# Wider modulation columns, another order of products and an earlier gate on the output weights, in an fp32 hybrid block on one core

## The chip, the cores and the metric

One NeuronCore of a Trainium2 chip runs the whole program. The metric is device time in microseconds (us). The kernel before took 2079.22 us, the median of 3 runs (2076.57 to 2082.44). A core has a matrix engine (PE, with its weight loads listed as PEld), three elementwise engines (DVE, ACT, POOL), and SP, which here only issues transfers; each takes its instructions in the order in which they are written for it, and waits on semaphores for the others.

## The reference

One layer on 1024 tokens with model width 1024, all in float32. The modulation vector is a product of the conditioning c with a 1024 x 6144 matrix, cut into six vectors of 1024.

```python
mod = c @ w_ada + b_ada       # shift, scale, gate for each of the two sub-layers
h = rms_norm(x) * (1 + scale) + shift
z = h @ w_in                  # q, k, v of both mixers, their gates, two branch gates
y_a = diff_attention(...)     # 8 heads, softmax(q1 k1) - lam * softmax(q2 k2), causal
y_b = mlstm_chunkwise(...)    # 4 heads
merged = sigmoid(g_A) * (y_a @ w_a) + sigmoid(g_B) * (y_b @ w_m)
x = x + gate * (merged @ w_out)
h2 = rms_norm(x) * (1 + scale2) + shift2
x = x + gate2 * (relu(h2 @ w_ff1) ** 2 @ w_ff2)     # width 4096
```

(The lines are a shortened form; `...` stands for the projected columns.)

## The kernel before

**Arithmetic.** Every float32 operand is split into a high and a low part (ACT copies the high part, line 320 in `parts`; DVE subtracts it, line 138), and a product is three matrix products: high by high, high by low, low by high (`mm_block`, line 328). Most large products use a scheme with seven block products instead of eight. Each left and right operand of the seven, named 1 to 7, is a block or a sum or difference of blocks, made on DVE before it is split; the results are added up on DVE as they come out of PSUM (lines 313 and 316 are the helpers `sub` and `add`). Products 1 and 2 give the first output block, 3 and 4 end the second and third, 6 or 7 the fourth.

**Stages, in order of time.** Input norm and the first modulation columns; from about 60 us the *token-major* units (`Tok`: five units of seven products of 48 matmuls with 256 columns) with the rest of the modulation woven in; then `Conv` and `Gate` units with 512 columns (from 306.92 us); the four mLSTM heads; the eight attention heads, with the products by w_m in the last; the products by w_a, the merge of both branches and the product by w_out (`Chunks`, seven products of 48 matmuls with 512 columns); the first feed-forward matrix in groups (`Ff1`, g0 to g15); the second one (28 products of 48 matmuls) with the residual added in.

**Modulation.** `ada_unit` makes 256 of the 4096 remaining columns: two loads of 512 KB into one buffer (`cr[1]`, named crow), eight DVE operations of 128x256 that multiply a row block with its entry of c and add (lines 715 and 717), a product with a matrix of ones that sums over the partitions (tile adp, lines 725 and 731). A load and all its eight operations are one entry of the list `extra`, put between two products; 14 of the 16 units fit there, two are put between the parts of the mLSTM heads.

**Order of work.** Nothing reorders instructions at run time: the order in which the Python functions call the engines is the order of each engine's queue. `weave` puts filler steps between main steps. Loads are issued from SP, in order as well: one that waits for a buffer holds up those behind it. Buffers come from pools by tag ("r", "v", "e", "u", "f", "m"); a new tile of a tag waits until the oldest one is free. `Chunks.prep` splits the operands of the next product, `Chunks.run` does the matmuls.

**Output gate.** The rows of w_out are loaded in pieces (line 1631) and multiplied by the gate (tile gta, line 1664) just ahead of the splits that use them. **Feed-forward.** A group's four result blocks are squared ReLUs; seven blocks or sums of them go to DRAM (act_d) as left operands of the second matrix. At the seam between the two matrices the first operands (act, tag "r") and the residual (xn_d, four loads of 1 MB into acc, line 2011) are loaded while the last group ends.

Of the kernel before, what the change touches and what calls it, by code (L numbers as in the profile page):

```python
# [36 lines left out]
def kernel(  # L37
# [40 lines left out]
    ub_d = dp.tile([AH, S + P], F32, name="ub_d")  # L78
    ea_d = dp.tile([32, S], F32, name="ea_d")
# [195 lines left out]
    def run(steps):  # L275
        for f in steps:
            f()
# [66 lines left out]
    class Group:  # L344
# [20 lines left out]

        def load_first(self):
# [32 lines left out]
        def weights(self, order):  # L399
# [3 lines left out]
            for q, i in enumerate(order):  # L403
# [7 lines left out]
                if i == 7:  # L411
# [200 lines left out]
    def gate_rows(gps):  # L612

        gs = wt("b", [16, S], "gs")
        for i in range(2):
            nc.scalar.copy(gs[:, i * 512:(i + 1) * 512], gps[i][0:16, :])
        nc.sync.dma_start(gs_d, gs)
# [77 lines left out]
    def ada_unit(u):  # L695

        c0 = 2048 + u * 256
        box = []

        def gather():  # L700
            ab = wt("f", [P, 2, 256], "ac")
            ac = ab[:, 0]
            box.append(ab)
            if u < 4 or u >= 12:
                nc.sync.dma_start(
                    ab[:, 1], bass.AP(tensor=b_ada.tensor, offset=b_ada.offset + c0, ap=[[0, P], [1, 256]])
                )
            src = w_ada[0][:, c0:c0 + 256].rearrange("(k p) c -> p k c", p=P)
            for q in range(2):
                stv = cr[1].rearrange("p (k c) -> p k c", k=4)  # L710
                nc.sync.dma_start(stv, src[:, q * 4:q * 4 + 4, :])
                for k in range(4):
                    kk = q * 4 + k
                    if kk == 0:
                        nc.vector.tensor_scalar(ac, stv[:, k, :], cond[:, 0:1], None, op0=ALU.mult)
                    else:
                        nc.vector.scalar_tensor_tensor(  # L717
                            ac, stv[:, k, :], cond[:, kk:kk + 1], ac, op0=ALU.mult, op1=ALU.add
                        )

        def total():
            ac, br = box[0][:, 0], box[0][:, 1]
            ps = bank("pa", "adp")
            if u < 4 or u >= 12:
                nc.tensor.matmul(ps[:, 0:256], lhsT=ones, rhs=ac, start=True, stop=True)
                nc.vector.tensor_tensor(br, ps[:, 0:256], br, op=ALU.add)
                i, cc = (0, u * 256) if u < 4 else (1, (u - 12) * 256)
# [97 lines left out]
    class Tok(Group):  # L825
# [13 lines left out]
        def s3(self):  # L839
            return cr[0].rearrange("p (k c) -> p k c", k=4)  # L840
# [1232 lines left out]
```

## Time and profile before

| what | value |
|---|---|
| median of 3 runs | 2079.22 us |
| the profiled execution's own time; its span; clock | 2075.06 us; 2073.0 us; 0.979 of full speed |
| PE busy | 1989.1 us, 96% of the span |
| DVE busy | 1655.4 us, 80% |
| ACT busy | 1045.0 us, 50% |
| POOL busy | 59.3 us, 3% |
| moved by DMA | 296.71 MB, mean 143 GB/s |

PE is nearly always busy by this count, but a matmul counts as busy for longer where the clock is low or where it follows a gap, so the count of matmuls in a stretch tells more than the busy share: in an undisturbed stretch with 512 columns there are 219 in 50 us, that is 0.228 us for each. The granted clock (PEclk) is 1.00 at 2.4 GHz and falls towards 0.5 at 1.2 GHz.

### The profile page before, as it was taken

To read this page: it belongs to the slowest core of one execution; us is meant where nothing else is said; L and a number is where in the kernel's file an instruction comes from. 1 tells how busy PE (TensorE), PEld (TensorE's weight loads), DVE (VectorE), ACT (ScalarE), POOL (GpSimd) and SP (SyncE) were. 2 spreads that over 40 slices of the span, in tenths; PEclk is the share of its full clock that TensorE was granted. 3 is DMA by queue.
4 is the path that set the end of the run, shared out by engine and by line. 5 is a ranking of instruction groups with operands and counts; after the bars stand their busy time and mean duration, and the time that the engine had idled before them with its cause. 6 is when DMAs were issued, how large, how long until landed. Compare 5 with 4: busy or idle time off the path is not lost.

```text
span 2073.0 us, 30238 instructions
## 1 busy us (share of the span) xinstructions
PE 1989.1 (96%) x11201; PEld 1723.2 (83%) x11201; DVE 1655.4 (80%) x2964; ACT 1045.0 (50%) x1966; POOL 59.3 (3%) x154
## 2 busy tenths in 40 slices
PE   5899999999999999999999899999899999999999
PEld 5899998888787899999999788777678887788887
DVE  7976768889676568999978657999867667998896
ACT  5522324544566557877767634456445445433332
POOL 0000000000011000000000110000000000000000
PEclk7999999999999999999999999999999999999999
DMA  8354452333765442322222665513444446744532
GB/s 283 107 173 157 146 180 101 102 112 134 219 207 169 138 126 54 85 77 82 62 64 85 198 226 168 185 41 112 162 153 153 146 148 235 275 154 159 163 107 77
DMA packets 210633, 296.71 MB, mean 143 GB/s; under 512 B 14067, under 2 KB 132494, under 8 KB 210486
## 3 DMA queue, kind: packets, MB, share of 16 engines
q1 hardware_dynamic: 207542, 285.35, 43.2%
q0 software_dynamic: 2944, 9.44, 1.2%
q8 instruction: 88, 1.44, 0.3%
q14 instruction: 59, 0.48, 0.1%
HBM read 206.43 MB, written 79.93 MB: 138 GB/s over the span
## 4 chain that ended last, share of the span: by engine, by line
PE 62%; DVE 15%; DMA 11%; issue 6%; ACT 4%; POOL 1%; SPq 0%; DVEq 0%; POOLq 0%; ACTq 0%
PE cps L328 15%; PE pb L328 8%; PE pc L328 7%; PE pa L328 7%; PE pd L328 4%; DMA crow<-in_w_ada_dram 4%; PE ps L166 3%; PE ps L165 3%; PE ps L167 3%; PE lg L1190 3%; PE pv L1243 3%; DVE ac L717 2%; DMA ex<-ea_d 1%; PE tp L1223 1%; PE ops L579 1%
## 5 line engine op out<-in xcount | busy, mean ns | idle before, releaser
L328 PE MATMUL cps<-t_op,s_op 128*128 128x512 f32 x2016 | 471.9, 395 | 10.6 <-ACT s_op L320 5.2
L328 PEld LDWEIGHTS cps<-t_op,s_op 128*128 128x128 f32 x2016 | 379.1, 189 | 100.8 <-ACT s_op L320 6.5
L320 ACT ACTIVATE w_op<-w_st 128x512 fp32r<-128x512 f32 (+1 forms) x192 | 130.6, 695 | 179.8 <-PE pb L328 62.6
L138 DVE TENSOR_TENSOR w_op<-w_st,w_op 128x512 fp32r<-128x512 f32 (+1 forms) x192 | 144.3, 770 | 8.3 <-ACT w_op L320 6.4
L165 PE MATMUL ps<-w_hi,hT 128*128 128x256 f32 x512 | 146.5, 286 | 0.0
L166 PE MATMUL ps<-w_lo,hT 128*128 128x256 f32 x512 | 145.9, 285 | 0.0
L167 PE MATMUL ps<-w_hi,hT 128*128 128x256 f32 x512 | 145.7, 284 | 0.0
L320 ACT ACTIVATE s_op<-act 128x1024 fp32r<-128x1024 f32 x56 | 58.6, 1052 | 143.4 <-PE cps L328 107.6
L328 PE MATMUL pc<-bt,w_op 128*128 128x512 f32 x384 | 99.8, 407 | 6.1 <-ACT w_op L320 5.1
L1200 ACT ACTIVATE ee<-ee,mneg 128x256 f32<-128x256 f32 (+7 forms) x128 | 98.2, 769 | 9.8 <-DVE mneg L1196 9.5
L1190 PE MATMUL lg<-kb,qe 128*128 128x512 f32 (+3 forms) x384 | 96.7, 360 | 3.2 <-DVE mneg L1196 2.5
L166 PEld LDWEIGHTS ps<-w_lo,hT 128*128 128x128 f32 x512 | 97.6, 191 | 1.3 <-issue 0.9
L165 PEld LDWEIGHTS ps<-w_hi,hT 128*128 128x128 f32 x512 | 97.6, 191 | 0.5
L167 PEld LDWEIGHTS ps<-w_hi,hT 128*128 128x128 f32 x512 | 97.6, 191 | 0.3
L328 PEld LDWEIGHTS pc<-bt,w_op 128*128 128x128 f32 x384 | 73.7, 195 | 27.2 <-ACT w_op L320 6.0
L328 PE MATMUL pa<-b,w_op 128*128 128x512 f32 x384 | 94.3, 396 | 0.7 <-DVE w_op L138 0.7
L316 DVE TENSOR_TENSOR acc<-cps,acc 128x512 f32<-128x512 f32 x116 | 76.9, 684 | 13.6 <-PE cps L328 13.5
L328 PEld LDWEIGHTS pa<-b,w_op 128*128 128x128 f32 x384 | 72.7, 190 | 16.1 <-DVE w_op L138 1.0
L717 DVE SCALAR_TENSOR_TENSOR ac<-crow,cond,ac 128x256 f32<-128x256 f32 x112 | 54.0, 482 | 29.5 <-DMA crow<-in_w_ada_dram 27.8
L1196 DVE CUSTOM_DVE_ANT_0 ee<-lg,bs 128x512 f32<-128x512 f32 (+4 forms) x128 | 69.9, 559 | 8.8 <-PE lg L1190 7.8
L138 DVE TENSOR_TENSOR s_op<-act,s_op 128x1024 fp32r<-128x1024 f32 x56 | 68.2, 1219 | 5.9 <-ACT s_op L320 5.9
L1190 PEld LDWEIGHTS lg<-kb,qe 128*128 128x128 f32 x384 | 61.5, 192 | 11.0 <-DVE mneg L1196 6.3
(406 smaller groups left out, 4798.8 us busy)
## 6 DMA issues: line engine op xcount, KB each, us to landing
w_st<-in_w_in_dram SPq DMA_DIRECT2D x72, 512.0 KB, 4.4
act<-act_d SPq DMA_DIRECT2D x56, 512.0 KB, 4.4
w_st<-in_w_ff_dram SPq DMA_DIRECT2D x36, 512.0 KB, 4.1
crow<-in_w_ada_dram SPq DMA_DIRECT2D x32, 512.0 KB, 4.2
w<-in_w_ff_dram SPq DMA_DIRECT2D x32, 512.0 KB, 4.9
act_d<-s SPq DMA_DIRECT2D x48, 256.0 KB, 2.0
wa<-in_w_ada_dram SPq DMA_DIRECT2D x16, 512.0 KB, 4.8
mq_d<-cv SPq DMA_DIRECT2D x16, 512.0 KB, 2.6
```

Source lines behind the costliest of these rows:

```text
L138: return (nc.gpsimd if pool else nc.vector).tensor_tensor(dst, src, hi.bitcast(F32), op=ALU.subtract)
L165: nc.tensor.matmul(o, lhsT=ah, rhs=bh, start=first, stop=False)
L166: nc.tensor.matmul(o, lhsT=ah, rhs=bl, start=False, stop=False)
L167: nc.tensor.matmul(o, lhsT=al, rhs=bh, start=False, stop=last)
L316: (nc.gpsimd if pick(pool, n) else nc.vector).tensor_tensor(o, a, b, op=ALU.add)
L320: nc.scalar.activation(dst[0], src, AF.Copy)
L328: nc.tensor.matmul(ps, lhsT=p, rhs=q, start=first and k == 0 and r == 0, stop=k == 3 and r == 2, skip_group_check=True,)
L717: nc.vector.scalar_tensor_tensor(ac, stv[:, k, :], cond[:, kk:kk + 1], ac, op0=ALU.mult, op1=ALU.add)
L1190: nc.tensor.matmul(lg[:, 0:max(256, w)], lhsT=hd["q"][hf][e][:, r, q4 * P:(q4 + 1) * P], rhs=hd["k"][e][:, c0:c0 + max(256, w)], start=r = ...
L1196: nc.vector.tensor_tensor_reduce(ee[:, c0:c0 + w], lg[:, 0:w], hd["bs"][:, n - c0 - w:n - c0][:, ::-1], -0.125, first, ALU.add, ALU.min, last,
L1200: nc.scalar.activation(ee[:, 0:n], ee[:, 0:n], AF.Exp, bias=mneg[:, e:e + 1], scale=-1.0, accum_out=ssum[:, e:e + 1])
L1243: nc.tensor.matmul(pv[:, 0:256], lhsT=pts[kk // 4][r][:, (kk % 4) * P:(kk % 4 + 1) * P], rhs=v, start=kk == 0 and r == 0, stop=kk == qi an ...
```

## The change

Six places are edited.

1. *Modulation.* Eight units of 512 columns. A load of 512 KB now holds two row blocks of 512 columns; the loads go to two buffers in turn, each is issued two products before its two DVE operations (128x512), and the product by ones comes one product after the last of them. All 32 loads lie in the token-major stage and the first `Conv` unit; the mLSTM heads have none. Where the gate needs its bias, this is a load of its own.
2. *Token-major units.* Products in the order 1, 2, 5, 6, 3, 7, 4; the left operand of 7 is made in place of a block; product 5's result is copied by ACT. The first unit's loads and splits stand between the calls that make its right operands.
3. *Output weights.* During the last attention head the rows of w_out are loaded (8 x 512 KB, buffer "u"), multiplied by the gate on DVE and stored to wo_d; later `pieces` loads from there.
4. *First feed-forward matrix, start.* For g0 to g3 the square of the first block is made by ACT; g0's and g1's sums of blocks are made two at a time in groups 6 and 8 from reloaded blocks; all eight evictions of the second half of the normed input go to ACT.
5. *Last group.* Order 1, 6, 5, 3, 7, 4, 2; its sums are made after the second matrix's ninth product.
6. *Residual.* The four loads of xn_d go; after the 10th, 11th, 12th and 14th of the second matrix's 28 products, POOL issues one transfer of 1 MB each that adds it to an accumulator in place (`accum_op`). The first seven products go in the order 1, 2, 7, 4, 5, 6, 3, and their results are copied by ACT where nothing is to be added.

```diff
@@
+        def fetch(q):
+            stv = cr[q % 2].rearrange("p (k c) -> p k c", k=2)
+            src = w_ada[0][q * 256:(q + 1) * 256, c0:c0 + 512].rearrange("(k p) c -> p k c", p=P)
+            nc.sync.dma_start(stv, src)
...
+            for k in range(2):
+                f = cond[:, q * 2 + k:q * 2 + k + 1]
+                if q or k:
+                    nc.vector.scalar_tensor_tensor(ac, stv[:, k, :], f, ac, op0=ALU.mult, op1=ALU.add)
+                else:
+                    nc.vector.tensor_scalar(ac, stv[:, k, :], f, None, op0=ALU.mult)
@@
+        def p5(self):
+            for n in self.ns:
+                self.pb[n] = bank("pa", "pb5")
+                self.m7[n] = wt("m", [P, 512], "m7")
+                self.prod(5, n, self.pb[n], True)
+                nc.scalar.activation(self.m7[n], self.pb[n], AF.Copy)
@@
     right(7, "vvvv")
+    first_tok.load()
     right(5, "eeee")
+    first_tok.weights(ORDER_T[0:2])
     half(1)
     gate_rows(gps)
     right(6, "rrrr")
+    first_tok.weights(ORDER_T[2:6])
     right(4, "rruu")
+    first_tok.weights(ORDER_T[6:])
...
+    for u, (fetch, gather, total) in enumerate(ada):
+        for q in range(4):
+            extra[2 + u * 4 + q].append(lambda f=fetch, q=q: f(q))
+            extra[4 + u * 4 + q].insert(0, lambda f=gather, q=q: f(q))
+        extra[8 + u * 4].insert(0, total)
@@
-        more = ada[na + h::MH]
-        for u, (gather, total) in enumerate(more):
-            filler.insert(len(filler) * (2 * u + 1) // (2 * len(more) + 1), gather)
-            filler.insert(len(filler) * (2 * u + 2) // (2 * len(more) + 1), total)
@@
+            def gate_wo(r):
+                w = wos.pop(r)
+                nc.vector.tensor_tensor(w, w, gta, op=ALU.mult)
+                nc.sync.dma_start(wo_d[r * P:(r + 1) * P, :], w)
+
+            for r in range(8):
+                units[12 + 2 * r] = lambda r=r, f=units[12 + 2 * r]: (fetch_wo(r), f())
+                units[15 + 2 * r] = lambda r=r, f=units[15 + 2 * r]: (gate_wo(r), f())
@@
-            wo = pieces("e", "wo", w_out[0], False, (11,), behind)
+            wo = pieces("e", "wo", wo_d, False, (11,))
@@
+        elif g.g in (6, 8):
+            fetch, one, two = late_sums(groups[LATE[g.g // 2 - 3]])
+            g.weights((1, 7, 2, 5, 6, 3, 4))
+            run([fetch, g.p1, g.p7, g.p2, g.p5, one, g.p6, two, g.p3, g.p4])
@@
-        if i == 1 and c == 0:
-            nc.scalar.activation(au[:, j], ps, AF.Copy)
+        if c == 0 and i not in (5, 6):
+            nc.scalar.activation(d[:, j], ps, AF.Copy)
@@
-    for q, t0, c0 in ((aa, 0, 0), (ab, 0, 512), (ac, 512, 0), (av, 512, 512)):
-        nc.sync.dma_start(q, xn_d[t0:t0 + 512, c0:c0 + 512].rearrange("(t p) c -> p t c", p=P))
...
+    joins = {9: ((aa, 0, 0),), 10: ((ac, 512, 0),), 11: ((av, 512, 512),), 13: ((ab, 0, 512),)}
     for n in range(7 * NC):
...
+        if n == 8:
+            groups[-1].sums()
+        for q, t0, c0 in joins.get(n, ()):
+            nc.gpsimd.dma_start(
+                q, xn_d[t0:t0 + 512, c0:c0 + 512].rearrange("(t p) c -> p t c", p=P), accum_op=ALU.add
+            )
```

DVE's queue before, in the first token-major unit: the modulation's operations (crow, cond to ac) between weight splits (w_op), weight sums (w_st) and result sums (m).

```order
L715 TENSOR_SCALAR ac<-crow,cond 128x256
L138 TENSOR_TENSOR w_op<-w_st,w_op 128x1024
L717 SCALAR_TENSOR_TENSOR ac<-crow,cond,ac 128x256 x3
L138 TENSOR_TENSOR w_op<-w_st,w_op 128x1024
L313 TENSOR_TENSOR crow<-w_st 128x1024
L316 TENSOR_TENSOR m_917<-pb_982,m_917 128x512
L717 SCALAR_TENSOR_TENSOR ac<-crow,cond,ac 128x256 x3
L316 TENSOR_TENSOR m_944<-pb_1008,m_944 128x512
L717 SCALAR_TENSOR_TENSOR ac<-crow,cond,ac 128x256
L316 TENSOR_TENSOR w_st<-w_st 128x1024
L138 TENSOR_TENSOR w_op<-w_st,w_op 128x1024
L316 TENSOR_TENSOR m_797<-pd,m_797 128x512
```

The same place in the changed kernel; the second product's split (w_op) already stands well ahead of these rows.

```order
L317 TENSOR_TENSOR c<-pb_907,m_800 128x512
L317 TENSOR_TENSOR c<-pb_934,m_827 128x512
L723 TENSOR_SCALAR ac<-crow,cond 128x512
L317 TENSOR_TENSOR w_st<-w_st 128x1024
L721 SCALAR_TENSOR_TENSOR ac<-crow,cond,ac 128x512
L139 TENSOR_TENSOR w_op<-w_st,w_op 128x1024
L317 TENSOR_TENSOR m_908<-pc,m_908 128x512
L721 SCALAR_TENSOR_TENSOR ac<-crow,cond,ac 128x512
L317 TENSOR_TENSOR m_908<-m_908,m_800 128x512
L317 TENSOR_TENSOR m_935<-pc,m_935 128x512
L721 SCALAR_TENSOR_TENSOR ac<-crow,cond,ac 128x512
L317 TENSOR_TENSOR m_935<-m_935,m_827 128x512
```

The operations are twice as wide and half as many, and one or two, not up to three or five, stand between two result sums.

DVE's queue before, at the end of the feed-forward groups g0 and g1: s are the sums that go to DRAM, s_15345 is the left operand of product 7 of g2, and its split (w_op) is what PE needs next.

```order
L316 TENSOR_TENSOR c<-c,m_15085 128x512
L316 TENSOR_TENSOR m_14855<-pc,m_14855 128x512
L313 TENSOR_TENSOR s_15270<-c,a_15227 128x512
L313 TENSOR_TENSOR s_15289<-a_15247,c 128x512
L313 TENSOR_TENSOR s_15270<-m_14855,s_15270 128x512
L316 TENSOR_TENSOR c<-c,m_15109 128x512
L316 TENSOR_TENSOR m_14870<-pc,m_14870 128x512
L313 TENSOR_TENSOR s_15294<-c,a_15247 128x512
L313 TENSOR_TENSOR s_15345<-w_st 128x512
L316 TENSOR_TENSOR w_st<-w_st 128x4x128
L313 TENSOR_TENSOR s_15294<-m_14870,s_15294 128x512
L138 TENSOR_TENSOR w_op<-s_15345,w_op 128x512
```

And now, where s_15254 is the left operand of product 7 of g2:

```order
L139 TENSOR_TENSOR w_op<-w_st,w_op 128x512
L317 TENSOR_TENSOR c<-pb_15082,m_14786 128x512
L139 TENSOR_TENSOR w_op<-w_st,w_op 128x512
L317 TENSOR_TENSOR c<-pb_15096,m_14801 128x512
L314 TENSOR_TENSOR s_15254<-w_st 128x512
L317 TENSOR_TENSOR w_st<-w_st 128x4x128
L139 TENSOR_TENSOR w_op<-s_15254,w_op 128x512
```

The sums and the second block's additions no longer stand between the last c of g1 and the operand of g2.

DVE's queue now, in the last attention head, where nothing of w_out stood before: wor is a row block of w_out, sg the products by w_m, ee, ssum and ptl the softmax.

```order
L1257 TENSOR_TENSOR ptl<-tp,pth 128x512
L1284 TENSOR_TENSOR yt<-yt,ssy 128x512
L1235 RECIPROCAL ssum<-ssum 128x2
L1257 TENSOR_TENSOR ptl<-tp,pth 128x128
L1236 SCALAR_TENSOR_TENSOR ssum<-ssum,nlam 128x1
L1541 TENSOR_TENSOR wor<-wor,gta 128x1024
L1239 SCALAR_TENSOR_TENSOR ee<-ee,ssum 128x768
L1541 TENSOR_TENSOR wor<-wor,gta 128x1024
L139 TENSOR_TENSOR w_lo<-w_st,w_hi 128x1024
L1320 SCALAR_TENSOR_TENSOR sg<-sg,ps 128x512
L139 TENSOR_TENSOR w_lo<-w_st,w_hi 128x1024
```

Each wor row waits for a load that was issued three steps earlier, and the softmax stands behind it.

## Rows read from the trace of the kernel before

**Rows 1.** The page: PE's busy time with its share of the span and instructions, and the shares of the chain that ended last, by engine.

```profile
PE 1989.1 (96%) x11201; PEld 1723.2 (83%) x11201; DVE 1655.4 (80%) x2964; ACT 1045.0 (50%) x1966; POOL 59.3 (3%) x154
...
PE 62%; DVE 15%; DMA 11%; issue 6%; ACT 4%; POOL 1%; SPq 0%; DVEq 0%; POOLq 0%; ACTq 0%
```

**Rows 2.** The view of windows, by stage: window, its length, then for PE, PEld, DVE, ACT and POOL the busy time (and instructions), the granted clock, the busy share of the DMA engines, GB/s.

```profile
60.00:310.00 250.00, 234.48 (x1853) 229.79 (x1852) 184.08 (x305) 76.81 (x108) 3.43 (x6) 0.96 0.50 155
310.00:540.00 230.00, 230.00 (x1016) 188.57 (x1015) 193.98 (x249) 108.35 (x155) 0.00 (x0) 1.00 0.39 131
...
1100.00:1180.00 80.00, 74.23 (x437) 64.46 (x437) 69.40 (x180) 58.67 (x137) 4.88 (x8) 0.94 0.47 146
1180.00:1300.00 120.00, 119.29 (x555) 98.66 (x554) 76.83 (x106) 49.92 (x79) 8.13 (x14) 1.00 0.59 195
1300.00:1400.00 100.00, 94.75 (x401) 75.35 (x400) 98.84 (x126) 46.41 (x66) 1.85 (x2) 0.98 0.32 108
1400.00:1500.00 100.00, 91.70 (x408) 73.22 (x407) 87.81 (x144) 55.84 (x102) 3.27 (x3) 0.95 0.41 137
...
1510.00:1740.00 230.00, 230.00 (x1001) 186.60 (x1000) 159.56 (x251) 114.53 (x189) 0.00 (x0) 1.00 0.44 151
1740.00:1800.00 60.00, 54.65 (x226) 42.56 (x225) 52.68 (x60) 27.43 (x34) 0.00 (x0) 0.97 0.88 313
...
1800.00:1850.00 50.00, 50.00 (x219) 40.86 (x218) 47.23 (x55) 19.32 (x22) 0.00 (x0) 1.00 0.52 168
```

**Rows 3.** The view of PE's waits from 60 to 310 us: what waited, for what; us in total, times, the longest.

```profile
PE pb L328 <- DVE m L316: 6.6, 2, 3.9
...
PE adp L731 <- DVE ac L717: 1.8, 2, 1.4
```

**Rows 4.** The same for DVE, from 60 to 310 us.

```profile
DVE ac L717 <- DMA crow<-in_w_ada_dram: 26.5, 12, 3.5
DVE ac L715 <- DMA crow<-in_w_ada_dram: 18.0, 9, 3.0
```

**Rows 5.** The view of windows, ten microseconds at the start of the token-major stage (columns as in group 2).

```profile
80.00:90.00 10.00, 4.05 (x25) 3.65 (x23) 10.00 (x14) 5.45 (x10) 0.00 (x0) 0.71 0.39 113
```

**Rows 6.** The timeline of PE at the start of the token-major stage: start, length, engine, line, operation, names and shapes, number, and in brackets the idle time before and what ended it.

```profile
75.56 6.02 PE L328 MATMUL pa<-w_op,hT 128*128 128x256 f32 x49
...
87.92 7.10 PE L328 MATMUL pa<-w_op,hT 128*128 128x256 f32 x46 [4.33 <-DVE w_op L138]
```

**Rows 7.** The same view at the end of the stage, where the first `Conv` product begins.

```profile
306.92 2.91 PE L328 MATMUL pa<-hT,w_op 128*128 128x512 f32 x12
```

**Rows 8.** The timeline of DVE at the start of the token-major stage.

```profile
78.08 1.09 DVE L604 TENSOR_SCALAR mo<-mo 128x512 f32<-128x512 f32 x3
...
86.64 1.22 DVE L138 TENSOR_TENSOR w_op<-w_st,w_op 128x1024 fp32r<-128x1024 f32 x1
```

**Rows 9.** The chain that ended last, in order of time (start, length, what), one whole product of the token-major stage.

```profile
203.99 5.77 PE pd L328 x48
```

**Rows 10.** The view of the tile crow: line, engine, operation, names, number: shortest, median, longest in ns, first and last start, shapes.

```profile
L717 DVE SCALAR_TENSOR_TENSOR ac<-crow,cond,ac x112: 474/484/487, 99.1 to 621.6; 128x256 f32<-128x256 f32 x112
L789 DVE SCALAR_TENSOR_TENSOR cv<-crow,par_v,cv x48: 1274/1278/1286, 326.0 to 508.0; 128x1023 f32<-128x1023 f32 x16, 128x1022 f32<-128x1022 f32 x16, 128x1021 f32<-128x1021 f32 x16
```

**Rows 11.** The view of the tile adp, columns as above.

```profile
L725 PE MATMUL adp<-ac,ksq x16: 377/377/484, 129.2 to 626.0; 128*128 128x256 f32 x16
```

**Rows 12.** The chain in the first mLSTM head.

```profile
567.81 3.95 DMA crow<-in_w_ada_dram
```

**Rows 13.** The view of line 1664, the output weights by the gate.

```profile
L1664 DVE TENSOR_TENSOR wo<-wo,gta x8: 1216/1226/1227, 1283.6 to 1329.3; 128x1024 f32<-128x1024 f32 x8
```

**Rows 14.** The view of windows in the last attention head.

```profile
1200.00:1210.00 10.00, 10.00 (x46) 8.27 (x45) 7.83 (x10) 3.82 (x6) 0.54 (x1) 1.00 0.99 348
```

**Rows 15.** PE's waits from 1300 to 1400 us.

```profile
PE cps L328 <- ACT t_op L320: 2.7, 1, 2.7
PE cps L328 <- DVE t_op L138: 2.5, 3, 1.5
```

**Rows 16.** PE's waits from 1400 to 1500 us, the two largest of g2's product 7 and 6.

```profile
PE pc L328 <- ACT w_op L320: 3.8, 1, 3.8
...
PE pd L328 <- ACT w_op L320: 1.1, 1, 1.1
```

**Rows 17.** The timeline of DVE there: the last c of g1, and the left operand of product 7 of g2.

```profile
1476.53 0.68 DVE L316 TENSOR_TENSOR c<-pb,m 128x512 f32<-128x512 f32 x1
...
1482.54 0.69 DVE L313 TENSOR_TENSOR s<-w_st 128x512 f32<-128x512 f32 x1
```

**Rows 18.** The view of windows there.

```profile
1480.00:1490.00 10.00, 6.25 (x16) 4.39 (x15) 8.83 (x15) 4.24 (x8) 0.00 (x0) 0.68 0.99 339
```

**Rows 19.** PE's waits from 1740 to 1800 us, the seam of the two feed-forward matrices.

```profile
PE cps L328 <- ACT s_op L320: 5.2, 3, 2.4
```

**Rows 20.** The chain at the seam.

```profile
1768.23 11.42 DMA act<-act_d
```

**Rows 21.** The page: transfers by queue (q0 holds those that POOL issues) with packets, MB and their share of 16 engines over the span.

```profile
q0 software_dynamic: 2944, 9.44, 1.2%
```

**Rows 22.** The page: transfers of one kind, with their number, KB each and us from issue to landing.

```profile
wo<-in_w_out_dram SPq DMA_DIRECT2D x8, 512.0 KB, 5.2
...
acc<-xn_d SPq DMA_DIRECT2D x4, 1024.0 KB, 9.4
```

More of the change, by code (lines that the diff above doesn't have):

```diff
@@ new lines, in gather @@
+        def gather(q):
+            stv = cr[q % 2].rearrange("p (k c) -> p k c", k=2)
+            if not q:
+                box.append(wt("f", [P, 512], "ac"))
+            ac = box[0]
+            for k in range(2):
[4 more added lines that the diff above has]
+                    nc.vector.tensor_scalar(ac, stv[:, k, :], f, None, op0=ALU.mult)
+            if gate and q == 3:
+                br = wt("f", [P, 512], "br")
+                nc.sync.dma_start(br, bass.AP(tensor=b_ada.tensor, offset=b_ada.offset + c0, ap=[[0, P], [1, 512]]))
+                box.append(br)
@@ L721, in total @@
         def total():
-            ac, br = box[0][:, 0], box[0][:, 1]
+            ac = box[0]
             ps = bank("pa", "adp")
[L724 to L727, printed above, removed]
-                nc.gpsimd.dma_start(gt_d[i, :, cc:cc + 256], br)
+            if gate:
+                br = box[1]
+                nc.tensor.matmul(ps, lhsT=ones, rhs=ac, start=True, stop=True)
+                nc.vector.tensor_tensor(br, ps, br, op=ALU.add)
+                i, cc = (0, u * 512) if u < 2 else (1, (u - 6) * 512)
+                nc.gpsimd.dma_start(gt_d[i, :, cc:cc + 512], br)
@@ L729, in total @@
             else:
-                for t in range(2):
+                for t in range(4):
                     nc.tensor.matmul(
@@ L1441 @@
         del behind[:]
-        u.all([lambda n=n: run(steps[n * len(steps) // 4:(n + 1) * len(steps) // 4]) for n in range(4)] + [lambda: None] * 3)
+        steps = [lambda v=steps[n * len(steps) // 4:(n + 1) * len(steps) // 4]: run(v) for n in range(4)]
+        u.all((extra[7 * len(toks):] if v == 0 else steps) + [lambda: None] * (4 if v == 0 else 3))
     run(behind)
@@ L1807, in out @@
                 c = wt("f", [P, 512], "c")
-            if b is None:
+            if b is None and self.g < 4:
+                nc.scalar.activation(c, a, AF.Relu)
+                nc.scalar.activation(c, c, AF.Square)
+            elif b is None:
                 nc.scalar.activation(c, a, AF.Relu)
@@ new lines, with late_sums, fetch, one @@
+    LATE = (0, 1)
+    def late_sums(g):
+        x, y = (wt("e", [P, 2, 512], "late") for _ in range(2))
+        a11, a21, a22, a12 = x[:, 0], x[:, 1], y[:, 0], y[:, 1]
+        def fetch():
+            for v, i in ((a11, 1), (a21, 5), (a22, 4), (a12, 2)):
+                nc.sync.dma_start(v, act_d[i][g.g * P:(g.g + 1) * P, :])
+        def one():
+            add(a22, a21, a22, False)
+            g.put(5, a22)
+            sub(a21, a11, a21, False)
+            g.put(7, a21)
+        def two():
+            sub(a11, a22, a11, False)
+            g.put(6, a11)
+            sub(a12, a12, a11, False)
+            g.put(3, a12)
+        return fetch, one, two
@@ L1961 @@
         else:
-            g.weights((1, 7, 2, 5, 6, 3, 4))
-            run([g.p1, g.p7, g.p2, g.p5, g.p6, g.p3, g.p4])
+            g.weights(ORDER_L)
+            run([getattr(g, f"p{i}") for i in ORDER_L])
     def out_f(c, i, j, ps):
```

180 lines of the change are left out of this document (122 added, 58 removed).

## The prediction

> **What bounds the kernel now.** I read the page first: PE is busy 1989.1 of 2073.0 us and has 62% of the chain that ended last, DVE 15%, DMA 11% [rows 1]. So PE is the bound, and time can be won only where PE stands or runs slowly. The windows by stage say where [rows 2]: the undisturbed rate is 219 matmuls of 512 columns in 50 us, 0.228 us each, and 310 to 540 us has no gap at all, so an edit there is worth nothing. Gaps lie in the token-major stage (234.48 busy of 250, clock 0.96), in 1100 to 1180, in the merge (94.75 of 100), at the feed-forward start (91.70 of 100) and at the seam (54.65 of 60). The sum is made against the profiled execution, 2075.06 us (2.06 us lie around its span); that is 4.16 us under the median, so its gains are taken off 2079.22.
>
> **Part 1 and 2: modulation and token-major units.** PE's waits here are few, 6.6 us for result sums and 1.8 us for the modulation's own sum [rows 3], and yet the stage loses far more. The reader is to see why in DVE's queue: it stands 26.5 + 18.0 us waiting for crow [rows 4], because the one buffer makes each load start only when the operations before it are done, and the sums and splits that PE needs stand behind them. PE's share of such a delay is booked under many names and under the clock.
> I therefore count products, not waits. The first product starts at 75.56 [rows 6]; the first `Conv` product at 306.92 [rows 7]: 231.4 us. A full product of 48 matmuls takes 5.77 us [rows 9], 35 of them 202.0. The matmuls by ones take 0.377 us for 256 columns [rows 11] and come in pairs; 512 columns at twice that, four gate units and four units of small ones come to about 6 us as an estimate. Left over as loss: 231.4 - 202.0 - 6 = 23.4 us.
> What goes: at the start PE stands 4.33 us to 87.92 for the second weight split [rows 6], with a window at clock 0.71 and 25 matmuls [rows 5]. That split starts at 86.64, behind operands of products 6 and 4; the changed order puts it where DVE stands at 78.08 [rows 8], so product 2 follows product 1. Next is product 5: ahead of its split stand the operand of product 6 and its own sum, about as much as DVE does from 78.08 to 86.64 [rows 8], so it is ready near 88, when product 2 ends (75.56 + 2 x 5.77 = 87.1).
> Each load now has two products, 11.5 us, to land; one on the chain takes 3.95 us [rows 12]. Price on DVE: a 128x256 operation takes 484 ns, a 128x1023 one 1278 [rows 10], so 512 columns take about 0.75 us by the line through both; 64 of them are 48 us against 16 x 8 x 0.48 = 61 before, and ten result adds go to ACT. DVE has room (busy 184.08 of 250, [rows 2]). I leave 4.5 us of the 23.4 for waits at unit changes, where the next unit's first split still stands behind product 6's sums: gain 19 us, bounds 11 (half the loss stays) and 23.4 (none does).
> The mLSTM heads lose two units with four loads; the chain shows one of them at 3.95 us [rows 12]. Bounds 0 (hidden otherwise) and 8 (two such stalls); I take 2, near to none: beside the loads the heads have long chains of small steps that would then end last.
>
> **Part 3: output weights earlier.** Eight multiplications of 1.226 us [rows 13] leave 1283 to 1330 us and the first-needed split moves up. DVE is busy 98.84 of 100 us from 1300 on, and PE waits 2.7 + 2.5 us for t_op, the splits of these weights [rows 2, 15]. By their first and last start (1283.6 and 1329.3) some five of the eight lie behind 1300, where DVE no longer idles: 6 us, as much as PE waits. Gain 5, bounds 3 and 7.
> The same work goes into the last head: about 10 us of DVE, where DVE is busy 69.40 of 80 up to 1180 but only 76.83 of 120 behind it [rows 2]. By the order they stand among the softmax of the last two query blocks, two or three of them before DVE has room. Moved with them are 8 loads and 8 stores of 512 KB on SP's queue, ahead of the loads for the product by w_a; 8 MB at the 348 GB/s that DMA reaches there [rows 14] are 24 us of DMA in a stretch that is 0.59 busy for 120 [rows 2]: room for 49. Cost 2, bounds 0 and 8 (all of DVE's 10 us less its idle time before 1180).
>
> **Part 4: feed-forward start.** PE waits 3.8 and 1.1 us for g2's operands [rows 16], and the window holds 16 matmuls at clock 0.68 [rows 18] where 44 fit at 0.228. On DVE the last c of g1 starts at 1476.53, the operand of product 7 at 1482.54 [rows 17]: in the 6 us between stand the sums that the change puts off. Without them the operand is ready some 5 us earlier, more than the 4.9 waited. The window lost 28 matmuls, 6.4 us. What is late next is g3's product 7, whose place in the queue does not change. The late sums run between 1510 and 1740, where PE is busy 230 of 230 and DVE 159.56 [rows 2], so they are hidden; without that cover they cost 8 x 0.69. Gain 6, bounds 3 and 8.3 (all that PE is not busy there, [rows 2]).
>
> **Part 5 and 6: the seam.** From 1740 to 1800 us there are 226 matmuls against 263 at the full rate [rows 2]: 37 missing, 8.4 us. PE waits 5.2 us for the split of act [rows 19], and that for the load of act, 11.42 us on the chain [rows 20], in a stretch at 313 GB/s and DMA share 0.88 [rows 2]. The four residual loads of 1 MB, 9.4 us each to landing [rows 22], are the neighbours of that load: 4 MB of the 18.8 in these 60 us. They go, and the buffers for act come free after the second product of the last group. Gain 6, bounds 2 (the act loads still wait for buffers) and 8.4.
> An accumulating transfer is nowhere in this trace. From below it is 1 MB at the rate of POOL's queue, 9.44 MB in 1.2% of the span [rows 21], 2.8 us; from above twice the 9.4 us [rows 22], 19, since it reads and writes. The next adds to the same accumulator come seven products later, 7 x 48 x 0.228 = 77 us. I take 9.4; both ends are hidden.
> The Trainium skill speaks against a gain here: by "DMA: Bandwidth & Descriptors" (Issuing engines are not separate DMA queues) transfers started by POOL run on the same 16 DMA engines as SP's. So moving the residual to POOL alone would relieve nothing; it is the later time that helps, and the DMA share at 1800 to 1850 leaves it room (0.52, [rows 2]). The page's fit for POOL's path (Anatomy of one DMA) gives 4.4 us per MB as an estimate; by that too nothing waits.
>
> **Sum.** -19 - 2 - 5 + 2 - 6 - 6 = -36 us: 2039.1 for an execution like the profiled one, 2043.2 for the median. I forecast 2044. With the bounds reached in two or three parts at once, on either side, this case alone gives 2030 to 2056.
>
> **Rivals.**
> *The waits move on (about half the gain).* For it: DVE is busy 87.81 to 98.84 of 100 from 1300 to 1500 [rows 2], so a wait taken away may come back at the next product there, and the token-major stage's sums stay in one queue with the modulation. Against it: from 310 to 540 and from 1510 to 1740 PE is saturated with the same kind of queue [rows 2]. Then 11 + 0 - 2 + 3 + 3 + 3 = 18 us: 2061.
> *The output weights stall DVE in the last head (slower).* Each of the eight multiplications waits for its own load, and the softmax, the sums of w_m and the splits for w_a stand behind it in DVE's queue, while PE is busy 119.29 of 120 there [rows 2], so nothing is caught up. Such a load takes 5.2 us to landing [rows 22], more where DMA is at 0.99 [rows 14]. If each stands its whole landing, 8 x 5.2 = 41.6 us: 2043.2 + 41.6 - 2 = 2083. It decides from 4.5 us per multiplication (36 / 8). Against it: the load is issued three steps earlier, not just ahead of its use.
> *The clock gives more.* The windows with gaps have the low clock too (0.71, 0.68, [rows 5, 18]), so a gap removed also takes the slow matmuls behind it. With every upper bound but the heads': 23.4 + 3 + 7 + 8.3 + 8.4 = 50 us: 2029.
>
> **Chances.** Forecast 0.6, half the gain 0.22, slower 0.07, more 0.11. Range 2029 to 2066: the upper end takes the half case and a little of what lies over it, and leaves out under 2 in 10 on both sides. About 0.3%, 6.2 us, is what a measurement of this kernel can tell from no change: faster is under 2073. The forecast, the stronger case and nearly all of the half case lie there, 0.87; of the rest 0.06 fall within, 0.07 above.
>
> **What would show it.** Token-major: crow no longer in DVE's waits, the first `Conv` product near 288 shows the step right, at 298 or later half of it. Heads: no crow there. Last head: 1100 to 1300 with no new wait of PE for ee, pth or sg and none of DVE for wor; over 1 us for each wor would be the slow rival. Merge: no wait of PE for t_op. Feed-forward start: the window around g2 with 40 matmuls or more. Seam: act landing under 6 us, no wait for s_op, and no wait of DVE for the four transfers. Wrong would be the whole if DVE's queue, not the order in it, sets the pace: then PE's waits keep their sum under new names.

## The result and the profile after

The changed kernel takes 2056.25 us (median of 4 runs, 2055.94 to 2063.55) against 2080.32 us (the median of 4 runs now; the 2079.22 above is that of 3): ratio 0.9904, 95% interval 0.9886 to 0.9921, a gain of 24.1 us. It was forecast at 2044, with a range of 2029 to 2066. The profiled execution has a span of 2054.6 us, 18.4 less than before; the smaller difference is because the one profiled before, 2075.06 us, lies 5.3 under its median, and the one profiled now, 2056.41, at its median. The stages below are those of these two executions.

The same matmul can be found in both traces, since their number in each stage didn't change. The table gives the time between the first matmuls of successive stages.

| stage, by its first matmuls | before | after | difference |
|---|---|---|---|
| up to the first token-major product | 75.56 | 74.63 | -0.93 |
| token-major units | 231.35 | 208.00 | -23.35 |
| `Conv` and `Gate` units | 235.75 | 236.99 | +1.24 |
| mLSTM heads | 230.16 | 231.85 | +1.69 |
| attention heads 0 to 6 | 363.20 | 364.84 | +1.64 |
| last head, products by w_m and w_a | 194.65 | 200.78 | +6.13 |
| product by w_out, up to the feed-forward | 89.50 | 83.82 | -5.68 |
| first quarter of the first feed-forward matrix | 98.83 | 88.78 | -10.05 |
| most of the rest of it | 212.68 | 212.65 | -0.03 |
| seam, up to the fifth product of the second matrix | 72.09 | 64.31 | -7.78 |
| the other 24 products | 265.12 | 283.93 | +18.81 |

Up to the fifth product of the second matrix the changed kernel is 37.1 us ahead; in the rest it gives half of that back. The windows of the changed kernel by the same stages, columns as in [rows 2]:

```profile
60.00:285.00 225.00, 224.25 (x1838) 220.03 (x1837) 174.78 (x245) 76.29 (x106) 1.87 (x3) 1.00 0.59 181
...
1080.00:1160.00 80.00, 74.61 (x432) 64.07 (x432) 72.75 (x185) 55.59 (x132) 4.88 (x8) 0.94 0.60 193
1160.00:1285.00 125.00, 119.10 (x544) 97.90 (x543) 78.86 (x104) 50.41 (x80) 8.13 (x14) 0.99 0.66 228
1285.00:1380.00 95.00, 93.24 (x404) 75.29 (x403) 92.69 (x119) 47.30 (x67) 1.76 (x1) 1.00 0.31 108
1380.00:1480.00 100.00, 94.42 (x432) 75.99 (x431) 86.18 (x143) 64.47 (x119) 3.37 (x3) 0.98 0.40 132
...
1705.00:1765.00 60.00, 59.31 (x259) 48.09 (x258) 51.19 (x53) 35.10 (x50) 0.00 (x0) 1.00 0.84 287
1770.00:1850.00 80.00, 80.00 (x350) 65.27 (x349) 64.22 (x73) 29.80 (x34) 1.37 (x1) 1.00 0.55 171
1850.00:1900.00 50.00, 36.47 (x137) 28.71 (x136) 36.96 (x42) 11.89 (x14) 3.83 (x3) 0.83 0.60 154
1910.00:2040.00 130.00, 130.00 (x566) 106.08 (x565) 114.11 (x134) 43.14 (x46) 0.00 (x0) 1.00 0.35 115
```

The first `Conv` product now starts at 282.64 us (306.92 before, [rows 7]):

```profile
282.64 2.91 PE L329 MATMUL pa<-hT,w_op 128*128 128x512 f32 x12
```

The token-major stage has no gap left (224.25 of 225, clock 1.00; 234.48 of 250 at 0.96 before). The seam holds 259 matmuls in 60 us where 226 stood. The new hole is 1850 to 1900: 137 matmuls where 219 fit, clock 0.83. By the starts of the products it is the 14th that takes 27.4 us instead of 10.9, and the 15th 13.4 instead of 11.2; the others of these 24 take what they took before, within 0.2 us. This is no scatter: seven executions of kernels with the same second matrix, the changed one among them, take 282.9 to 284.7 us for the last row of the table. Who waits there, for the changed kernel from 1850 to 1920 us:

```profile
POOL acc L2177 <- DVE acc L317: 59.0, 3, 26.8
...
DVE w L2093 <- DMA w<-in_w_ff_dram: 17.3, 4, 6.5
...
PE cps L329 <- DVE acc L317: 7.8, 1, 7.8
...
PE cps L329 <- DVE t_op L139: 5.7, 1, 5.7
```

DVE waits for w, the second matrix's blocks, and PE for DVE. PE's timeline has both waits, at the start of the 14th and of the 15th product:

```profile
1872.43 13.48 PE L329 MATMUL cps<-t_op,s_op 128*128 128x512 f32 x47 [5.74 <-DVE t_op L139]
1893.69 18.52 PE L329 MATMUL cps<-t_op,s_op 128*128 128x512 f32 x70 [7.78 <-DVE acc L317]
```

The two waits are 13.5 of the 18.8 us. The other 5 are the matmuls behind them: 47 in 13.48 us and 70 in 18.52, where 0.228 each would make 10.7 and 16.0; the granted clock was 0.66 from 1870 to 1880 us and 0.58 from 1890 to 1900. The chain from 1840 to 1915 us (start, length, what) and POOL's timeline from 1780 to 1912 us:

```profile
1838.43 11.68 DMA w<-in_w_ff_dram
...
1856.60 10.53 DMA w<-in_w_ff_dram
...
1872.41 10.49 DMA w<-in_w_ff_dram
...
1893.69 21.47 PE cps L329 x83
```

```profile
1835.56 1.37 POOL L2177 DMA_DIRECT2D acc<-xn_d  x1 [428.59 <-ACT t_op L321]
1853.47 1.30 POOL L2177 DMA_DIRECT2D acc<-xn_d  x1 [16.54 <-DVE acc L317]
1870.41 1.27 POOL L2177 DMA_DIRECT2D acc<-xn_d  x1 [15.64 <-DVE acc L317]
1898.51 1.26 POOL L2177 DMA_DIRECT2D acc<-xn_d  x1 [26.83 <-DVE acc L317]
```

Each of the three loads of w on this chain is issued some 2 to 3 us after an accumulating transfer and takes 10.5 to 11.7 us; the page's median for the loads of w is 5.4. The transfers themselves land late too (the line of their source: shortest, median, longest). And the DMA share of the ten microseconds behind the first transfer is 0.93, where the mean from 1770 to 1850 us is 0.55:

```profile
w<-in_w_ff_dram SPq DMA_DIRECT2D x32, 512.0 KB, 5.4
...
DMA to landing us min/median/max: 10.6/12.7/13.5
...
1840.00:1850.00 10.00, 10.00 (x46) 8.16 (x45) 1.83 (x2) 3.90 (x4) 0.00 (x0) 1.00 0.93 238
```

The fourth transfer, at 1898.51, has no load of w beside it, and no product that starts after it is longer than before.

In the kernel before the loads of w have no lead to lose, that is no time between their landing and the moment when DVE wants them: from 1855 to 1930 us DVE already waits 6.0 us for w in six places, the longest 1.9. SP waits for the split that frees the buffer (t_op) before it issues a load of w, 21 times from 1800 to 2060 us:

```profile
DVE w L1946 <- DMA w<-in_w_ff_dram: 6.0, 6, 1.9
...
SPq L1941 <- DVE t_op L138: 20.8, 21, 2.2
```

### The profile page after: what moved, and what is told of

It reads as the page before. It is cut to its first block, busy times and chain, and to the rows that moved or that the text cites. A ratio compares the mean times of both kernels' runs of the same rounds, so it can differ in the third digit from the quotient of the medians.

```text
span 2054.6 us, 30199 instructions
## 1 busy us (share of the span) xinstructions
PE 1980.4 (96%) x11193; PEld 1717.1 (84%) x11193; DVE 1629.2 (79%) x2867; ACT 1058.3 (52%) x1991; POOL 63.4 (3%) x154
## 4 chain that ended last, share of the span: by engine, by line
PE 76%; DVE 8%; DMA 7%; issue 4%; ACT 3%; POOL 1%; SPq 0%; POOLq 0%; DVEq 0%; ACTq 0%
PE cps L329 18%; PE pa L329 10%; PE pc L329 10%; PE pb L329 9%; PE pd L329 5%; PE ps L167 4%; PE ps L166 4%; PE ps L168 4%; PE lg L1220 3%; PE pv L1273 3%; DMA w<-in_w_ff_dram 2%; DMA ex<-ea_d 1%; PE tp L1253 1%; PE ops L586 1%; DMA xt<-in_x_dram 1%
## 5 line engine op out<-in xcount | busy, mean ns | idle before, releaser
L321 ACT ACTIVATE w_op<-w_st 128x512 fp32r<-128x512 f32 (+1 forms) x197 | 135.9, 705 | 197.7 <-PE pb L329 61.1
L139 DVE TENSOR_TENSOR w_op<-w_st,w_op 128x512 fp32r<-128x512 f32 (+1 forms) x197 | 150.2, 782 | 28.3 <-ACT w_op L321 26.4
L317 DVE TENSOR_TENSOR acc<-cps,acc 128x512 f32<-128x512 f32 x100 | 66.7, 684 | 12.8 <-PE cps L329 12.7
L2093 DVE TENSOR_TENSOR w<-w,gtf 128x1024 f32<-128x1024 f32 x32 | 39.0, 1223 | 40.3 <-DMA w<-in_w_ff_dram 37.0
```

Source lines behind the costliest of these rows:

```text
L139: return (nc.gpsimd if pool else nc.vector).tensor_tensor(dst, src, hi.bitcast(F32), op=ALU.subtract)
L317: (nc.gpsimd if pick(pool, n) else nc.vector).tensor_tensor(o, a, b, op=ALU.add)
L321: nc.scalar.activation(dst[0], src, AF.Copy)
L2093: nc.vector.tensor_tensor(t, t, g.unsqueeze(1).to_broadcast([P, 2, 512]), op=ALU.mult)
```

## The experiments

Twelve kernels ran. The edits are against the changed kernel unless another is named. Stage times are taken as in the table; its last row is called the second matrix's stage.

**Residual transfers as plain loads.**

```diff
-                q, xn_d[t0:t0 + 512, c0:c0 + 512].rearrange("(t p) c -> p t c", p=P), accum_op=ALU.add
+                q, xn_d[t0:t0 + 512, c0:c0 + 512].rearrange("(t p) c -> p t c", p=P)
```

> Changed kernel with the four residual transfers at their places and on the same queue, but as plain loads that overwrite the accumulator instead of adding (so the first products' sums are lost). Theory 1a (1 MB of anything beside the loads of w is enough): the stall stays within 4 us of 18.8, time 2052 to 2057. Theory 1b (adding makes the transfer slow and holds the DMA engines longer): the transfer lands in 5 to 9 us instead of 10.6 to 13.5, the stall falls under 8 us, time 2038 to 2046.

2046.72 us (2042.89 to 2049.15). The transfers land in 5.5 to 8.4 us, and the second matrix's stage takes 274.58 us: of the 18.8 us 9.5 stay. DVE's longest wait for w is 4.0 us instead of 6.5:

```profile
DMA to landing us min/median/max: 5.5/7.6/8.4
...
DVE w L2093 <- DMA w<-in_w_ff_dram: 11.7, 5, 4.0
```

So half of the stall is the 4 MB themselves and the other half the adding. Neither theory had this number, and the time lies between their ranges.

**Two transfers later.**

```diff
-    joins = {9: ((aa, 0, 0),), 10: ((ac, 512, 0),), 11: ((av, 512, 512),), 13: ((ab, 0, 512),)}
+    joins = {9: ((aa, 0, 0),), 13: ((ab, 0, 512), (ac, 512, 0)), 18: ((av, 512, 512),)}
```

> Changed kernel, but the accumulating transfers of two of the four residual blocks are issued later: the first stays after the 10th product of the second feed-forward matrix, two go together after the 14th and one after the 19th, instead of after the 10th, 11th, 12th and 14th. Theory 1 (the transfers slow the loads of w and act that are in flight beside them, three collisions in a row use up the lead): the 18.8 us that PE stands near the 14th and 15th product go but for 0 to 4, time 2037 to 2043. Theory 2 (the new order at the seam makes SP issue the loads of w too late, whatever POOL transfers): the stall stays, 2054 to 2058. Theory 3 (the adds themselves wait for the transfers to land): the stall moves to the 16th to 19th product and keeps 10 us or more, 2048 to 2058.

2056.49 us, as theories 2 and 3 had it, but the trace shows that the edit didn't do what it says (aa, ab, ac and av in the diff are the four accumulators). POOL's timeline:

```profile
1856.86 1.29 POOL L2177 DMA_DIRECT2D acc<-xn_d  x1 [16.51 <-DVE acc L317]
1896.20 1.27 POOL L2177 DMA_DIRECT2D acc<-xn_d  x1 [38.04 <-DVE acc L317]
```

The second transfer was issued at 1856.86 us, one product and a half after the first. That can't be the one for ab, which waits for the 14th product (it ends at 1891 us); it is the one for ac, which is ready after the 11th and is written behind that for ab. So the built program had a transfer that was ready ahead of one that had to wait. (The sentence ahead of the prediction that the order of the calls is the order of the queues is therefore too strong: for these two, without a dependency between them, it doesn't hold.) Three transfers still met loads of w, the last one later, and the stage took 285.51 us. By the starts of the products the 14th and 15th are now 12.4 us too long and the 21st and 22nd, where the moved transfer went, 7.8. One collision left the first place and the stall shrank there by a third, which speaks for theory 1; by its time the run decides nothing, the next two do.

**No residual at all.**

```diff
-    joins = {9: ((aa, 0, 0),), 10: ((ac, 512, 0),), 11: ((av, 512, 512),), 13: ((ab, 0, 512),)}
+    joins = {}
```

> Changed kernel without the four residual transfers (so the output lacks the residual of the feed-forward sub-layer). Theory 1 (all of the stall at the 14th and 15th product comes from the transfers beside the loads of w): no stall, 18 to 19 us less than the changed kernel, 2036 to 2040. Theory 2 (a part of the 9.5 us that stayed with plain loads comes from the new order at the seam): 4 to 9.5 us of stall stay, 2041 to 2048.

2038.88 us, and the second matrix's stage takes 265.39, as before the change (265.12). All of the stall comes from the transfers; nothing of it from the new order at the seam.

**Transfers in the gaps between the loads of w.** A one-column operation ties each tile to the last result of the 14th or 21st product, so that no transfer can be put ahead of it.

```diff
+    joins = {13: ((av, 512, 512),), 20: ((aa, 0, 0), (ac, 512, 0), (ab, 0, 512))}
...
+            if q is not ab:
+                nc.vector.scalar_tensor_tensor(
+                    q[:, 0, 0:1], ab[:, 3, 0:1], 0.0, q[:, 0, 0:1], op0=ALU.mult, op1=ALU.add
+                )
```

> Changed kernel with the residual transfers held back by a one-column DVE operation that reads the last result of the 14th and of the 21st product: one transfer behind the 14th, three behind the 21st, where no load of w is in flight. All is computed as before. Theory 1 (only the collision costs): 2036 to 2042, no stall over 2 us in the second feed-forward matrix, w landing in 4 to 6 us throughout. Theory 3 (an accumulating transfer stops the adds to its tile whenever it lands): stalls of 5 to 15 us near the 16th or the 23rd product, 2044 to 2054.

2037.88 us (2036.39 to 2044.53), ratio to before 0.9816 (0.9777 to 0.9855), with all of the computation: the best kernel here. POOL's timeline with the landing of its four transfers, and DVE's and PE's waits in the second matrix:

```profile
1881.46 1.37 POOL L2181 DMA_DIRECT2D acc<-xn_d  x1 [475.56 <-PE cps L329]
1958.06 3.87 POOL L2181 DMA_DIRECT2D acc<-xn_d  x3 [75.23 <-DVE acc L2178]
...
DMA to landing us min/median/max: 10.3/14.0/22.1
```

```profile
DVE w L2093 <- DMA w<-in_w_ff_dram: 11.2, 10, 2.0
DVE acc L317 <- DMA acc<-xn_d: 8.4, 1, 8.4
```

```profile
PE cps L329 <- DVE t_op L139: 0.6, 1, 0.6
PE cps L329 <- DVE acc L317: 0.3, 1, 0.3
```

No single wait for w is over 2.0 us. One add waits 8.4 us for the three transfers that go together, and the 25th product takes 12.4 us instead of 11.2. The stage takes 266.85 us. Theory 1 holds: the collision is the cost, and its size is 17 us (by this run) to 19 (by the one without transfers).

**Output weights back in their place.** The gate and its eight multiplications stand again ahead of the w_out product, and the last head has none of it.

```diff
-            wo = pieces("e", "wo", wo_d, False, (11,))
+            wo = pieces("e", "wo", w_out[0], False, (11,), behind)
```

> Changed kernel with part 3 alone undone: the output weights are gated just ahead of their splits, as before, and the last attention head has neither their loads and stores nor the eight multiplications. Theory A (part 3 costs the 7.8 us that the last attention head lost and gives the 5.7 us that the merge won): 2054 (2052 to 2056), the last head 7 to 8 us shorter, the stretch of the w_out product 5 to 6 longer. Theory B (the last head lost its time because everything before it came 21 us earlier, not by part 3): the last head stays, the w_out product loses 5.7, time 2061 to 2063.

2056.35 us, 0.35 over the range of theory A. The last head's stage takes 195.71 us (194.65 before, 200.78 changed) and the w_out product's 89.27 (89.50 and 83.82). Eight executions of kernels with the same last head, the changed one among them, take 200.8 to 202.7 us for it. By the stages theory A holds, with 5.1 and 5.5 us: the price and the gain of part 3 cancel.

**The last head without the multiplications, and without the transfers.**

```diff
-                nc.vector.tensor_tensor(w, w, gta, op=ALU.mult)
```

> Changed kernel whose last attention head loads and stores the rows of w_out as it does, but doesn't multiply them (the output weights stay without their gate). Theory E (DVE's eight multiplications cost the last head's 7.8 us): the head is 6 to 8 us shorter, up to the first product by w_a. Theory F (the 16 transfers and their place on SP's queue cost it): it is 0 to 2 us shorter.

2057.19 us; the stage takes 200.71, no shorter. In the other kernel the loads and stores go and the operation stays:

```diff
-                nc.sync.dma_start(wos[r], w_out[0][r * P:(r + 1) * P, :])
...
-                nc.vector.tensor_tensor(w, w, gta, op=ALU.mult)
-                nc.sync.dma_start(wo_d[r * P:(r + 1) * P, :], w)
+                nc.vector.tensor_tensor(gta, gta, gta, op=ALU.max)
```

> Changed kernel whose last attention head does eight DVE operations of the same size (a maximum of the gate tile with itself) at the same places, without loads and stores; the output weights are loaded later from the input and stay without their gate. Theory E (DVE): the head keeps 6 to 8 us of its loss. Theory F (transfers): the loss goes but for 0 to 2 us.

2048.17 us; the stage takes 194.51, as before the change. DVE's ten microseconds are free, and the transfers cost all of it: theory F. With 8 MB less, DMA's share from 1160 to 1240 us is 0.58 at 197 GB/s; the last line is the same stretch of the changed kernel:

```profile
1080.00:1160.00 80.00, 74.75 (x435) 63.79 (x434) 75.43 (x188) 57.03 (x133) 4.87 (x8) 0.96 0.50 155
1160.00:1240.00 80.00, 78.79 (x378) 65.30 (x377) 49.94 (x70) 26.38 (x47) 8.11 (x14) 1.00 0.58 197
...
1160.00:1240.00 80.00, 74.10 (x348) 61.19 (x347) 47.60 (x66) 25.18 (x45) 7.59 (x13) 0.98 0.73 257
```

Through which wait the transfers reach PE stays open: the waits there change their names from kernel to kernel.

**Who issues the stores.** On top of join_gap:

```diff
-                nc.sync.dma_start(wo_d[r * P:(r + 1) * P, :], w)
+                nc.gpsimd.dma_start(wo_d[r * P:(r + 1) * P, :], w)
```

> join_gap with the eight stores of the gated output weights issued by POOL instead of SP. Theory G (in SP's queue each store waits for its multiplication and holds up the loads behind it, which the last attention head needs): the head loses under 3 us of its 7.8, time 2031 to 2035. Theory H (8 MB more on the DMA engines in that stretch is what slows the loads, whoever issues them): the head keeps 6 us or more, 2036 to 2040.

2042.61 us; the last head's stage takes 205.39 us against 202.52 in join_gap. Moving the stores off SP wins nothing, so G's forecast falls; the time is over H's range as well. The edit had a price of its own: DVE waits 8.5 us for the rows in three places, where it waits 3.5 in join_gap. So what SP's queue costs by itself isn't shown, and H stays argued.

**The gating in the heads 2 to 5.** On top of join_gap, the row and the gate are loaded and multiplied at the end of each of these heads.

```diff
+            if 1 < h < 6:
+                for r in (h * 2 - 4, h * 2 - 3):
+                    filler += [lambda r=r: fetch_wo(r), lambda: None, lambda r=r: gate_wo(r)]
```

> join_gap with the gating of the output weights moved to the attention heads 2 to 5, two rows of blocks in each, at the end of each head's other work, where DMA is busy 0.26 and PE saturated; the gate is loaded anew for each row, so there are 4 MB more of loads. Theories G and H both: the last head is 7 us shorter than in join_gap and the heads 2 to 5 lose nothing, time 2029 to 2033. Rival: loads and multiplications hold up the softmax there as they do in the last head, 1 us or more for each of the eight, 2038 to 2046.

2062.54 us, over every forecast. The last head's stage comes down to 195.89, but the heads 0 to 6 take 394.08 instead of 365.22: the rival in kind, but at 3.6 us for each row block. From 750 to 1250 us PE waits for the softmax (mneg, 11.3 us in ten places), and the queries' raw tiles wait twice, 2.9 us in all, for the rows' multiplications, whose buffers they share; which of the two sets the price wasn't taken apart.

**One modulation buffer.**

```diff
-            stv = cr[q % 2].rearrange("p (k c) -> p k c", k=2)
+            stv = cr[1].rearrange("p (k c) -> p k c", k=2)
...
-            extra[2 + u * 4 + q].append(lambda f=fetch, q=q: f(q))
+            extra[4 + u * 4 + q].insert(0, lambda f=fetch, q=q: f(q))
```

> Changed kernel whose modulation loads use one buffer instead of two and are issued just ahead of their DVE operations, as before; the columns stay 512 wide and the order of products stays changed. Theory K (the two buffers and the early issue win the token-major stage): DVE waits again 2 us or more for most of the 32 loads and the stage is 10 to 20 us longer, 2066 to 2076. Theory L (half as many, wider operations and the order of products win it): under 6 us longer, 2056 to 2062.

2069.09 us (2065.9 to 2074.31). The token-major stage takes 218.25 us, 10.25 longer (twelve executions of kernels that keep the two buffers take 208.0 to 209.3), and `Conv` and `Gate` 6.3 longer. DVE's waits for crow in this kernel from 60 to 310 us (first fence) and in the changed one from 60 to 285 (second):

```profile
DVE ac L721 <- DMA crow<-in_w_ada_dram: 23.9, 17, 3.4
...
DVE ac L723 <- DMA crow<-in_w_ada_dram: 11.8, 7, 2.6
```

```profile
DVE ac L721 <- DMA crow<-in_w_ada_dram: 7.4, 7, 2.2
```

Theory K holds at its lower end, with 24 waits of 1.5 us in the mean, less than the 2 it named: the second buffer and the early issue are 10 of the stage's 23 us (and more behind it); the others are the start, the order and the wider operations, which weren't taken apart.

**The feed-forward start, two halves.** First the sums of g0 and g1 at once, as before, then instead the squares and four evictions back on DVE.

```diff
-                if 1 < self.g < 4:
+                if self.g < 4:
...
-            elif self.g in LATE:
-
-                self.put(5 if (t, hf) == (0, 1) else 2, c)
```

> Changed kernel with one edit of part 4 undone: the sums of g0 and g1 are made at once, as before, and groups 6 and 8 reload nothing. The squares of g0 to g3 and the evictions stay on ACT. Theory C (the sums in front of g2's operand were all of the 10 us won at the feed-forward start): the wait before g2's product 7 comes back, 8 to 10 us, 2064 to 2067. Theory D (the moved squares and evictions carry half of it): 3 to 6 us, 2059 to 2063.

```diff
-            if b is None and self.g < 4:
-                nc.scalar.activation(c, a, AF.Relu)
-                nc.scalar.activation(c, c, AF.Square)
...
-    feat1 = norm_feat(range(4, 8), range(8), b_at)
+    feat1 = norm_feat(range(4, 8), (4, 5, 6, 7), b_at)
```

> Changed kernel with the squares of g0 to g3 and the evictions of the second half of the normed input back as before (squares and four of eight evictions on DVE); the late sums stay. Theory M (with late_back's 4 us these make up the 10 us of the feed-forward start): 5 to 7 us longer there, 2061 to 2064. Theory N (DVE's queue has room once the sums are gone): 0 to 2 us, 2056 to 2058.

2059.35 and 2057.2 us. The first quarter of the matrix takes 92.73 and 92.19 us, 3.9 and 3.4 more than the changed kernel's 88.78; in the executions of the other kernels, whose code is the same there, it takes 88.1 to 91.9. So each half is worth at most some 4 us alone, neither carries the 10, and both lie less than 1 us over that scatter: theory C falls, D is the nearest, and between M and N it stays open. The two together leave some 3 of the 10 us without an owner.

## Why the prediction was right in sign and too large in size

*The sum.* By the medians 24.1 us were gained where 36 were forecast. In the profiled executions the change was 37.1 us ahead by the fifth product of the second matrix, and then 18.8 us went to something that the sum had at nothing. In the kernel where only that is mended, 2037.88 us was measured. That 37.1 lies so near to 36 is luck: the token-major stage, the merge, the feed-forward start and the seam gained 10.9 us more than forecast, and the `Conv` units, the mLSTM heads and the attention heads cost 10.7 more. It is luck, too, that the time lies inside the range: its upper end was set for a rival that didn't come true.

*The step that failed* is the last of parts 5 and 6: "I take 9.4; both ends are hidden." A landing of 9.4 us was too low (10.6 to 13.5), but that isn't the error: no instruction of the changed kernel waits for one of the four to land, so from the adds it was hidden, as the step says. The transfer was priced by who reads what it writes, and not by who loads beside it. Its neighbours are the loads of w, which have no lead. I had read the mean DMA share of 0.52 as room, and a mean share says nothing of how long one load takes beside a transfer that is in flight. The rule of the Trainium skill that was cited, "DMA: Bandwidth & Descriptors" (Issuing engines are not separate DMA queues), speaks of it: the transfers of POOL and SP share the engines and interleave. The trace agrees: loads of w at 10.5 to 11.7 us where 5.4 is their median; whether they met in the engines or in the memory, no run here shows. I used the rule for bytes alone. By the fit that the Trainium skill gives for POOL's path ("DMA: Bandwidth & Descriptors", Anatomy of one DMA) 1 MB would take 4.4 us, as an estimate; measured here are 5.5 at the shortest without adding (join_plain) and 10.3 with it (join_gap).

*Token-major stage*, -19: it came to -23.35, the upper bound (23.4). The waits at unit changes that I kept 4.5 us for didn't come; PE waits in one place, 0.7 us. The waits for crow fell from 44.5 us [rows 4] to 7.4. And the second product now follows the first at once, as PE's timeline shows (columns as in [rows 6]): 96 matmuls in one row, product 5 behind them.

```profile
74.63 11.66 PE L329 MATMUL pa<-w_op,hT 128*128 128x256 f32 x96
86.14 5.96 PE L329 MATMUL pb<-w_op,t 128*128 128x256 f32 x48
```

*mLSTM heads*, -2: +1.7 in the profiled execution. Twelve executions of kernels whose code is the same there, the changed one among them, take 227.5 to 234.5 us, with a mean of 230.2, and it took 230.16 before: the term came to nothing, and the stall read from one chain row was no gain.

*Part 3.* The merge was right, -5.68 for -5; PE's wait for t_op there fell from 5.2 us to 1.8. The last head was at the upper bound, +7.8 with the heads before it, where I took 2, and for another reason: the step named DVE's ten microseconds, and wo_nodma shows them free. The step's "room for 49" is the same error as at the seam: bytes were compared with a mean share. The rival of the output weights stalling DVE fell too: DVE waits 2.6 us in all for the eight loads.

```profile
DVE wor L1541 <- DMA wor<-in_w_out_dram: 2.6, 4, 1.4
```

*Feed-forward start*, -6: -10.05, over the bound of 8.3, which was PE's idle time; the slow matmuls behind each gap came back with it (16 matmuls at clock 0.68 in the ten microseconds of [rows 18], 45 at clock 1.00 from 1450 to 1460 us in the changed kernel, where the same products run). *Seam*, -6: -7.78, near its upper bound.

*The rivals.* In the sum for "the clock gives more" the mLSTM heads stand at 3 us, which their step doesn't give (it has 0, 2 and 8); nothing here rests on it. The time is that of "the waits move on", 2061, more than that of the forecast, but not its mechanism: the waits that were taken away stayed away, and what is missing was lost in one place where PE had not waited.

## What to carry to other kernels

Before a transfer is moved into a stretch, look at the loads that run there and at how much lead each has when its reader comes: a reader that already waits a little in several places, for loads issued only as buffers come free, has no lead, and a transfer beside them goes onto the path though it is on another queue: here 1 MB at a time on POOL's queue, 9.5 us for four without adding and 18.8 with it. Move transfers into stretches without such loads, and tie them there by a data dependence, since without one they can be pulled forward, as in join_late. A price for a transfer needs two numbers, its own landing and what it adds to the landing of its neighbours.

## What the runs showed of the hardware

An accumulating transfer of 1 MB from DRAM into SBUF takes 10.6 to 13.5 us to land beside other loads (10.3 in join_gap with no load of w in flight), the same transfer without adding on the same queue 5.5 to 8.4. The pages of the changed kernel and of join_plain show what the queue held of the engines, for the same bytes with and without adding:

```profile
q0 software_dynamic: 4992, 13.63, 2.4%
...
q0 software_dynamic: 3968, 13.63, 1.8%
```

Against [rows 21], 9.44 MB and 1.2%, there are 4.19 MB more. With adding they take 1.2% of 2054.6 us, some 25 us of all 16 engines or 5.9 us per MB; without it 0.6% of 2041.1, some 12 us or 2.9 per MB. (The shares are rounded to 0.1%, so these are good to about a tenth and a sixth.) Three accumulating transfers issued together landed after 10.6, 17.5 and 22.1 us.
